# Where the weights of a split-float32 decoder block lie in SBUF: hi 192 bytes further in, everything else on multiples of 512 bytes

## The chip, the cores and the metric

The kernel runs on one core of a Trainium2 chip, with the other cores idle. The metric is the device time of one execution in microseconds (us). Before the change it is 1701.79 us, the median of 3 runs that lay between 1701.62 and 1701.97 us.

## What is computed

One layer of a hybrid decoder block on 256 tokens of width 2048, all in float32. The work is a chain of large products with the stages between them; the weights (about 320 MB) are read from HBM once.

```python
proj = x @ w_in                       # columns: gq gk gv gr glr | fq fk fv ff | ma mb
o  = gla_chunked(q, k, v, log_a)      # branch A: gated linear attention, 4 heads
y_gla = (rmsnorm(o) * silu(gr)) @ w_branch_gla
of = fox_attention(fq, fk, fv, log_f) # branch B: softmax attention with forget bias, 8 heads
y_fox = of @ w_branch_fox
x = layer_norm(ALPHA * x + (sigmoid(ma) * y_gla + sigmoid(mb) * y_fox) @ w_out)
g = causal_dwconv(x @ w_gate, conv_w, conv_b)
x = layer_norm(ALPHA * x + (gelu(g) * (x @ w_up)) @ w_down)
x = x + sigmoid(x @ w_ple_gate) * (p @ w_ple_proj)
```

## The kernel before

**Split numbers.** TensorE multiplies in float32r. So that the result keeps float32's accuracy, each operand is split into a rounded part `hi` and a remainder `lo = raw - hi`, and a product is three: weight-hi by x-hi, weight-hi by x-lo, and weight-lo by x-hi. A tile of activations holds both parts side by side: `a[:, kt%4, 0:256]` is hi of 256 tokens, `256:512` is lo.

**Units of weights.** All weights but the first stage's come in 284 units `u` of 128 x 2048, each as two halves of 128 x 1024. `prep()` makes a half: SyncE's queue (SP) loads it into `raw` (a ring of 4), ScalarE copies it into `hi` (L101), VectorE subtracts to make `lo` (L127). `unit()` hands out the next unit and keeps three prepared ahead. There are 6 places for `hi` and 6 for `lo`. Only SP and a few stretches of TensorE follow an order written out by hand; the other engines' order is the scheduler's.

**Two ways to multiply.** Where *weights are stationary* (176 units: fq, fk, gq, gk, ma, mb, the branch projections, gate and up; tiles `psfq psfk psq psk psm psa psb psg psu`), `w_unit` loads 128 columns of hi into the array, streams 512 columns of activations through them (L190), loads 128 columns of lo and streams 256 (L192): one pair for each 128 rows of the product, 16 pairs a unit. Nearly all of them, 173 units with 2768 pairs, run so; the first three of gate and up go by `w_phase`, 256 columns at a time. Where *activations are stationary* (108 units, `u` in 32-63, 120-135 and 224-283: gv, gr, `wo`, `dn`, `pg`), `x_mm` loads 128 columns of activations for each matmul and streams 512 columns of weights: for each of 128 rows of the product and each half of the tokens x-hi by hi (two matmuls), x-hi by lo (two), x-lo by hi (two), all at L234. That makes 24 matmuls a unit, 2592 in all; the last `pg` bank takes 256 columns at a time in its 96. In both ways every matmul has a weight load of its own, which TensorE takes while the matmul before it runs (PEld in the profile).

**The first stage** makes fv and two small pieces (glr and ff, 24 columns) with activations stationary from 1048 columns of weights, in three chunks `fch` of 352, 352 and 344 columns that lie behind each other in `fvhi` and `fvlo` (`big` places of 8192 bytes). `fv_prep` loads them into the `raw` ring, 8 units of two halves.

**Where tiles lie.** SBUF has a stretch of bytes in each of the 128 partitions; pools are laid out one behind the other in the order of the code. A weight load reads 128 columns of 4 bytes, which is 512 bytes, and a row of an activation tile is 2048 bytes, so a tile's place modulo 512 bytes is that of all its blocks. In the built programs the places modulo 512 are:

| tiles | before | after |
|---|---|---|
| hi, weights stationary | 0 | 192 |
| hi, activations stationary | 0 | 0 |
| lo | 64 | 0 |
| activations, pw, pTs, vs, fvhi, fvlo (`big`) | 0 | 0 |
| hT10, the last of dn's 11 activation tiles (`late`) | 128 | 0 |
| chunks of the first stage's weights | 0, 384, 256 | 0, 0, 0 |
| raw ring, four places | 0, 96, 192, 288 | 0, 0, 0, 0 |
| t1, t2 (small work tiles; ath and atl, the stationary tiles of `go`, among them) | 384 | 0 |
| ones | 64 | 416 |

Of the kernel before, what the change touches and what calls it, by code (L numbers as in the profile page):

```python
# [9 lines left out]
F32 = mybir.dt.float32  # L10
F32R = mybir.dt.float32r
# [8 lines left out]
P = 128  # L20
# [6 lines left out]
FH = 8  # L27
# [5 lines left out]
NS = 1048  # L33
# [4 lines left out]
AFF_DVE = (0, 2)  # L38
LN_ORDER = (1, 0, 3, 2)
GROWS = 96  # L40
PAD = 88
S8W = 2048

OFF = dict(gq=0, gk=1024, gv=2048, gr=4096, glr=6144, fq=6160, fk=7184, fv=8208,
           ff=9232, ma=9240, mb=11288)
# [3 lines left out]
def tile_block(ctx: ExitStack, tc: tile.TileContext, wu, wfv, wpp, xT_in, x_in, pT_in, wlr,  # L49
# [1 line left out]
    nc = tc.nc  # L51

    cst = ctx.enter_context(tc.tile_pool(name="cst", bufs=1))
    wide_hi = ctx.enter_context(tc.tile_pool(name="wide_hi", bufs=6))
    step = ctx.enter_context(tc.tile_pool(name="step", bufs=1))
    gap0 = step.tile([P, 16], F32, name="gap0")
    wide_lo = ctx.enter_context(tc.tile_pool(name="wide_lo", bufs=6))
    step2 = ctx.enter_context(tc.tile_pool(name="step2", bufs=1))
    gap1 = step2.tile([P, 112], F32, name="gap1")
    big = ctx.enter_context(tc.tile_pool(name="big", bufs=15))  # L60
    ring = ctx.enter_context(tc.tile_pool(name="ring", bufs=4))
    sm = ctx.enter_context(tc.tile_pool(name="sm", bufs=2))
# [6 lines left out]
    chn = cst.tile([P, chan.shape[1]], F32, name="chn")  # L69
    ident = cst.tile([P, P], F32, name="ident")  # L70
    mhalf = cst.tile([P, 1], F32, name="mhalf")
    pad = cst.tile([P, PAD], F32, name="pad")

    def s8(shape, dt=F32, name=None):
        t = big.tile([P, S8W], dt, tag="S8", name=name)
        n = int(np.prod(shape[1:]))
        t = t[:shape[0], :n]
        if len(shape) == 3:
            return t.rearrange("p (a b) -> p a b", b=shape[2])
        if len(shape) == 4:  # L80
            return t.rearrange("p (a b c) -> p a b c", b=shape[2], c=shape[3])
        return t

    def w_tile(tag, dt, name):
        pool = wide_hi if tag == "hi" else wide_lo
        return pool.tile([P, 1024], dt, tag=tag, name=name)

    def t1(name):
        return sm.tile([P, 256], F32, tag="t1", bufs=6, name=name)

    def t2(name):
        return sm.tile([P, 512], F32, tag="t2", bufs=6, name=name)

    def mmtile(name):
        return pmm.tile([P, 512], F32, tag="mm", name=name)
# [4 lines left out]
    def copy(o, i, scale=1.0):  # L100
        nc.scalar.activation(o, i, AF.Copy, bias=0.0, scale=scale)  # L101
# [15 lines left out]
    def prep():  # L117
        u = n_prep[0]
        n_prep[0] += 1
        his, los = [], []  # L120
        for h in range(2):
            raw = ring.tile([P, 1024], F32, tag="raw", bufs=4, name=f"raw{u}_{h}")
            nc.sync.dma_start(raw, wu[u, :, h * 1024:(h + 1) * 1024])
            hi = w_tile("hi", F32R, f"hi{u}_{h}")
            copy(hi, raw)
            lo = w_tile("lo", F32R, f"lo{u}_{h}")
            nc.vector.tensor_tensor(lo, raw, hi.bitcast(F32), ALU.subtract)  # L127
            his.append(hi)
            los.append(lo)
        ready[u] = (his, los)  # L130
# [4 lines left out]
    def unit():  # L135
        u = n_used[0]
        n_used[0] += 1
        while n_prep[0] < min(NU, u + 3):
            prep()
        return ready.pop(u)  # L140
# [161 lines left out]


    fv = s8([P, 2, 1024], name="fv")
    fch = ((0, 352), (352, 352), (704, 344))
    fbk = [[mmtile(f"fv_{t}{c}") for c in range(3)] for t in range(2)]

    def fv_prep(u, hs=(0, 1), his=None, los=None):
        his, los = his or [], los or []
        for h in hs:  # L310
            raw = ring.tile([P, NS], F32, tag="raw", bufs=4, name=f"fvraw{u}_{h}")
            hi = s8([P, NS], F32R, name=f"fvhi{u}_{h}")
            lo = s8([P, NS], F32R, name=f"fvlo{u}_{h}")
            for o, n in fch if u == 0 else ((0, NS),):
                e = slice(o, o + n)
                nc.sync.dma_start(raw[:, e], wfv[u, :, h, e])
                copy(hi[:, e], raw[:, e])
                nc.vector.tensor_tensor(lo[:, e], raw[:, e], hi[:, e].bitcast(F32), ALU.subtract)
            his.append(hi)
            los.append(lo)  # L320
        return his, los

    load_x(0, 0, 1, 1)
    f0 = fv_prep(0, (0,))
    load_x(0, 1, 2, 1)
    fvu = [fv_prep(0, (1,), *f0)]
    load_x(0, 2, 4)
    fvu.append(fv_prep(1))
    load_x(1, 0, 4)
    for u in range(8):  # L330
        hi, lo = fvu[u]
        for j in range(2):
            kt = 2 * u + j
            a = xT[kt // 4][:, kt % 4, :]
            for cs in ((0,), (1,), (2,)) if u == 0 else ((0, 1, 2),):
                for t in range(2):
                    ah, al = a[:, t * P:t * P + P], a[:, 256 + t * P:256 + t * P + P]
                    for i, (w, x) in enumerate(((hi[j], ah), (lo[j], ah), (hi[j], al))):
                        for c in cs:
                            o, n = fch[c]  # L340
# [20 lines left out]
    for t in range(2):  # L361
        tk = t1("smtok")
        nc.gpsimd.memset(tk, 0.0)
        for i in range(3):
            copy(tk[:, 32 * i:32 * i + 16], fbk[t][2][:, 320:336])
        copy(tk[:, P:P + FH], fbk[t][2][:, 336:344])
        nc.tensor.transpose(smp[:GROWS, t * P:t * P + P], tk[:, 0:GROWS], ident)
        nc.tensor.transpose(smp[:FH, 256 + t * P:256 + t * P + P], tk[:, P:P + FH], ident)
    for t in range(2):
# [147 lines left out]
    for nm, dst, sc in (("fq", fq, P ** -0.5), ("fk", fk, 1.0)):  # L517
        if nm == "fk":
            mixers.append(fox_gen())
        for n in range(8):  # L520
            hi, lo = unit()
# [8 lines left out]
    for nm, dst, sc in (("q", gq, 1.0 / 16.0), ("k", gk, 1.0)):  # L530
        for n in range(8):
            hi, lo = unit()
            ps = mmtile(f"ps{nm}{n}")
            w_unit(ps, hi, lo, xT, range(16), True, True)
            h, c = n // 2, n % 2
# [163 lines left out]
    for n in range(32):  # L699
        hi, lo = unit()  # L700
# [7 lines left out]
        pull(1)  # L708
    early.close()
    late = ctx.enter_context(tc.tile_pool(name="late", bufs=1))  # L710


    mT = [s8([P, 4, 512], F32R, name=f"mT{i}") for i in range(4)]
    fhl = None
    for n in range(16):
        hi, lo = unit()
# [162 lines left out]
        return banks  # L879

    z1 = [s8([P, 2048], name=f"z1{t}") for t in range(2)]
    st1 = [sm.tile([P, 4, 6], F32, tag=f"st1{t}", bufs=1, name=f"st1{t}") for t in range(2)]
    gain = [None, None]

    def mid1():
# [82 lines left out]
    tc.keep_in_program_order(nc.scalar.preload_act_table_set("gelu_apprx_tanh_and_others"))  # L968


    gp = [late.tile([P, 264], F32, name=f"gp{i}") for i in range(2)]
    for i in range(2):
        nc.gpsimd.memset(gp[i][:, 0:2], 0.0)
    hT = [None] * 11
# [12 lines left out]
    for n in range(NF):  # L987
# [17 lines left out]
        u = t1("up")  # L1005
# [6 lines left out]
            pull(1)  # L1012

    z2 = [s8([P, 2048], name=f"z2{t}") for t in range(2)]
    st2 = [sm.tile([P, 4, 6], F32, tag=f"st2{t}", bufs=1, name=f"st2{t}") for t in range(2)]

    def mid2():
        for t in range(2):
# [127 lines left out]
```

## Time and profile before

| what | value |
|---|---|
| median of 3 runs | 1701.79 us |
| the profiled execution | 1702.23 us, span 1699.5 us from first to last instruction |
| TensorE matmul busy | 1690.2 us, 99% of the span |
| TensorE weight loads busy | 1456.4 us, 86% |
| VectorE / ScalarE / GpSimd busy | 65% / 49% / 2% |
| DMA queues' share of 16 engines | 58.8% for SP's queue, mean 194 GB/s |
| granted TensorE clock | full all through |

How to read it: the duration of a matmul in a row (392 ns for one of 512 columns) is longer than the distance from its start to the next one's, since matmuls overlap in the array; what one costs is the distance between starts. In a timeline, rows of like matmuls that follow each other are merged with their count (x4), and the distance is the start of the next row less the start of this one, by the count. In a table of stretches, the number of matmuls (x433) takes in those that reach over an edge; as a matmul lasts less than twice the distance of two starts, two are taken off before dividing.

### The profile page before, as it was taken

The numbers are of one execution on the slowest core, as the hardware profiler recorded it, in microseconds if no ns is written. First come the engines' busy times: TensorE is split into PE (matmuls) and PEld (weight loads), VectorE is DVE, ScalarE is ACT, GpSimd is POOL, SyncE is SP. The second block draws the span as 40 slices with busy tenths as digits, with TensorE's granted clock in tenths as the row PEclk, the third lists the DMA queues.
The fourth block names the chain that finished last, engine by engine and source line by source line (L and its number), as shares of the span: only waits on it lengthen the run. The fifth ranks groups of instructions, "written<-read, shape, count | busy, mean of one in ns | idle before, by whom it ended". The sixth has DMA issues, their size and how long they took to land.

```text
span 1699.5 us, 23843 instructions
## 1 busy us (share of the span) xinstructions
PE 1690.2 (99%) x9035; PEld 1456.4 (86%) x9035; DVE 1098.0 (65%) x1588; ACT 833.9 (49%) x1200; POOL 36.7 (2%) x123
## 2 busy tenths in 40 slices
PE   9999999999999999999999999999999999999998
PEld 8888888888888888888888888888888888888787
DVE  6666658758756547774687776666666644544774
ACT  5655545445555544443365445445445433334633
POOL 0100000000000000000010000000000000000000
PEclk9999999999999999999999999999999999999999
DMA  7765555555555556557656665555555575566455
GB/s 266 260 198 166 165 185 180 178 175 178 181 174 173 162 187 192 190 189 281 220 165 197 215 215 191 192 190 188 188 195 188 191 287 189 187 194 199 158 175 172
DMA packets 91427, 330.22 MB, mean 194 GB/s; under 512 B 10232, under 2 KB 11904, under 8 KB 89904
## 3 DMA queue, kind: packets, MB, share of 16 engines
q1 hardware_dynamic: 90528, 324.51, 58.8%
q0 software_dynamic: 784, 4.20, 0.7%
q8 instruction: 70, 1.15, 0.3%
q14 instruction: 45, 0.37, 0.1%
HBM read 323.42 MB, written 5.25 MB: 193 GB/s over the span
## 4 chain that ended last, share of the span: by engine, by line
PE 98%; DVE 1%; ACT 0%; DMA 0%; SPq 0%; issue 0%; POOL 0%; ACTq 0%
PE dn L234 14%; PE psu L190 9%; PE psg L190 9%; PE psm L190 7%; PE gv L234 5%; PE gr L234 5%; PE pg L234 5%; PE wo L234 5%; PE psu L192 5%; PE psg L192 5%; PE psm L192 4%; PE psa L190 3%; PE fv L341 2%; PE psa L192 2%; PE psq L190 2%; PE psfk L190 2%
## 5 line engine op out<-in xcount | busy, mean ns | idle before, releaser
L127 DVE TENSOR_TENSOR lo<-raw,hi 128x1024 fp32r<-128x1024 f32 x568 | 694.2, 1224 | 506.9 <-ACT hi L101 505.7
L101 ACT ACTIVATE hi<-raw 128x1024 fp32r<-128x1024 f32 x568 | 601.7, 1060 | 732.6 <-issue 274.7
L190 PE MATMUL psu<-x1T,hi 128*128 128x512 f32 x688 | 240.4, 392 | 0.0
L190 PE MATMUL psg<-x1T,hi 128*128 128x512 f32 x672 | 234.8, 392 | 0.0
L192 PE MATMUL psu<-x1T,lo 128*128 128x256 f32 x688 | 192.3, 280 | 0.0
L234 PE MATMUL dn<-hi,hT 128*128 128x512 f32 x704 | 192.1, 392 | 0.0
L192 PE MATMUL psg<-x1T,lo 128*128 128x256 f32 x672 | 187.8, 280 | 0.0
L190 PE MATMUL psm<-xT,hi 128*128 128x512 f32 x512 | 179.8, 395 | 0.0
L234 PEld LDWEIGHTS dn<-hi,hT 128*128 128x128 f32 x704 | 132.1, 188 | 30.6
L190 PEld LDWEIGHTS psu<-x1T,hi 128*128 128x128 f32 x688 | 129.2, 188 | 27.6
L190 PEld LDWEIGHTS psg<-x1T,hi 128*128 128x128 f32 x672 | 126.2, 188 | 27.0
L192 PE MATMUL psm<-xT,lo 128*128 128x256 f32 x512 | 143.2, 280 | 0.0
L192 PEld LDWEIGHTS psu<-x1T,lo 128*128 128x128 f32 x688 | 130.6, 190 | 0.0
L192 PEld LDWEIGHTS psg<-x1T,lo 128*128 128x128 f32 x672 | 127.6, 190 | 0.0
L190 PEld LDWEIGHTS psm<-xT,hi 128*128 128x128 f32 x512 | 96.2, 188 | 21.2
L234 PE MATMUL dn<-lo,hT 128*128 128x512 f32 x352 | 111.9, 395 | 0.0
L192 PEld LDWEIGHTS psm<-xT,lo 128*128 128x128 f32 x512 | 97.0, 189 | 0.2
L190 PE MATMUL psa<-oT,hi 128*128 128x512 f32 x256 | 89.5, 392 | 0.0
L234 PEld LDWEIGHTS dn<-lo,hT 128*128 128x128 f32 x352 | 66.1, 188 | 14.8
L234 PE MATMUL gv<-hi,xT 128*128 128x512 f32 x256 | 72.6, 395 | 0.0
L234 PE MATMUL gr<-hi,xT 128*128 128x512 f32 x256 | 72.4, 395 | 0.0
L192 PE MATMUL psa<-oT,lo 128*128 128x256 f32 x256 | 71.6, 280 | 0.0
(247 smaller groups left out, 2435.2 us busy)
## 6 DMA issues: line engine op xcount, KB each, us to landing
raw<-in_wu_dram SPq DMA_DIRECT2D x568, 512.0 KB, 4.6
fvraw<-in_wfv_dram SPq DMA_DIRECT2D x14, 524.0 KB, 6.5
lnb<-in_lng_dram SPq DMA_DIRECT2D x4, 1024.0 KB, 13.3
z<-in_x_dram SPq DMA_DIRECT2D x2, 1024.0 KB, 9.5
praw<-in_wpp_dram SPq DMA_DIRECT2D x4, 512.0 KB, 4.5
x1d<-z POOLq DMA_DIRECT2D x2, 1024.0 KB, 7.6
z<-x1d SPq DMA_DIRECT2D x2, 1024.0 KB, 9.6
xraw<-in_xT_dram SPq DMA_DIRECT2D x7, 256.0 KB, 7.1
```

What stands on the lines that cost most here:

```text
L101: nc.scalar.activation(o, i, AF.Copy, bias=0.0, scale=scale)
L127: nc.vector.tensor_tensor(lo, raw, hi.bitcast(F32), ALU.subtract)
L190: nc.tensor.matmul(ps, lhsT=hi[i // 8 if hoff == 0 else 0][:, w0 % 1024:w0 % 1024 + P], rhs=a[:, kt % 4, :], start=first and i == 0, stop= ...
L192: nc.tensor.matmul(ps[:, 256:512], lhsT=lo[i // 8 if hoff == 0 else 0][:, w0 % 1024:w0 % 1024 + P], rhs=a[:, kt % 4, 0:256], start=False, ...
L234: nc.tensor.matmul(bs[j][:, 0:m], lhsT=x, rhs=v[:, o:o + m], start=first and i == 0, stop=last and i == 2)
L341: nc.tensor.matmul(fbk[t][c][:, 0:n], lhsT=x, rhs=w[:, o:o + n], start=kt == 0 and i == 0, stop=kt == 15 and i == 2)
```

## The change

One pool `wide` takes the place of two with gaps between them. A place for hi is now 1152 columns (4608 bytes) instead of 1024, and `w_tile` puts hi's 1024 columns 48 columns (192 bytes) into it unless `u` is in `XSTAT`, the units with activations stationary. lo, `big`, the ring, t1 and t2 come to 0 modulo 512. The first stage's raw rows move from the ring into hi's six places, its chunks become 384, 384 and 280 columns. Small tiles move so that all fits: statistics st1 and one of st2 to the constants, the convolution's rows gp into two of the six t2 places.

```diff
--- before.py
+++ after.py
...
-PAD = 88
+PAD = 16
+LPAD = 24
+XSTAT = (*range(32, 64), *range(120, 136), *range(224, 284))
 S8W = 2048
+WH = 1152
+HSTEP = 48
...
-    wide_hi = ctx.enter_context(tc.tile_pool(name="wide_hi", bufs=6))
-    step = ctx.enter_context(tc.tile_pool(name="step", bufs=1))
-    gap0 = step.tile([P, 16], F32, name="gap0")
-    wide_lo = ctx.enter_context(tc.tile_pool(name="wide_lo", bufs=6))
-    step2 = ctx.enter_context(tc.tile_pool(name="step2", bufs=1))
-    gap1 = step2.tile([P, 112], F32, name="gap1")
+    wide = ctx.enter_context(tc.tile_pool(name="wide", bufs=6))
     big = ctx.enter_context(tc.tile_pool(name="big", bufs=15))
...
+    st1 = [cst.tile([P, 4, 6], F32, name=f"st1{t}") for t in range(2)]
+    st20 = cst.tile([P, 4, 6], F32, name="st20")
     pad = cst.tile([P, PAD], F32, name="pad")
...
-    def w_tile(tag, dt, name):
-        pool = wide_hi if tag == "hi" else wide_lo
-        return pool.tile([P, 1024], dt, tag=tag, name=name)
+    def w_tile(tag, dt, name, u):
+        if tag == "lo":
+            return wide.tile([P, 1024], dt, tag=tag, name=name)
+        o = 0 if u in XSTAT else HSTEP
+        return wide.tile([P, WH], dt, tag=tag, name=name)[:, o:o + 1024]
...
-    fch = ((0, 352), (352, 352), (704, 344))
+    fch = ((0, 384), (384, 384), (768, 280))
...
-            raw = ring.tile([P, NS], F32, tag="raw", bufs=4, name=f"fvraw{u}_{h}")
+            raw = wide.tile([P, WH], F32, tag="hi", name=f"fvraw{u}_{h}")[:, 0:NS]
...
-            copy(tk[:, 32 * i:32 * i + 16], fbk[t][2][:, 320:336])
-        copy(tk[:, P:P + FH], fbk[t][2][:, 336:344])
+            copy(tk[:, 32 * i:32 * i + 16], fbk[t][2][:, 256:272])
+        copy(tk[:, P:P + FH], fbk[t][2][:, 272:280])
...
     late = ctx.enter_context(tc.tile_pool(name="late", bufs=1))
+    late.tile([P, LPAD], F32, name="lpad")
...
-    st1 = [sm.tile([P, 4, 6], F32, tag=f"st1{t}", bufs=1, name=f"st1{t}") for t in range(2)]
...
-    gp = [late.tile([P, 264], F32, name=f"gp{i}") for i in range(2)]
+    gp = [t2(f"gp{i}")[:, 0:264] for i in range(2)]
...
-    st2 = [sm.tile([P, 4, 6], F32, tag=f"st2{t}", bufs=1, name=f"st2{t}") for t in range(2)]
+    st2 = [st20, sm.tile([P, 4, 6], F32, tag="st2", bufs=1, name="st21")]
```

No instruction is added or taken away. In the order of the instructions two things are to be seen. The first is SP's queue in the first stage: `fvraw1_0` is unit 1's first half, and what stands in brackets is what SP waits for before it issues that load. Before:

```order
L316 DMA fvraw1_0_168<-in_wfv_dram 128x1048 [waits DMAHW1_49]
L316 DMA fvraw1_1_174<-in_wfv_dram 128x1048 [waits DMAHW2_49]
L149 DMA xraw_180<-in_xT_dram 128x512 [waits DMAHW3_49]
L149 DMA xraw_184<-in_xT_dram 128x512 [waits DMAHW4_49]
L316 DMA fvraw2_0_224<-in_wfv_dram 128x1048 [waits DMAHW5_49,DVE_49]
L316 DMA fvraw2_1_230<-in_wfv_dram 128x1048 [waits DMAHW7_49,DMAHW6_49,DVE_49]
```

After:

```order
L319 DMA fvraw1_0_160<-in_wfv_dram 128x1048 [waits DMAHW1_49]
L319 DMA fvraw1_1_166<-in_wfv_dram 128x1048 [waits DMAHW2_49]
L152 DMA xraw_172<-in_xT_dram 128x512 [waits DMAHW3_49]
L152 DMA xraw_176<-in_xT_dram 128x512 [waits DMAHW4_49]
L319 DMA fvraw2_0_216<-in_wfv_dram 128x1048 [waits DMAHW5_49]
L319 DMA fvraw2_1_222<-in_wfv_dram 128x1048 [waits DMAHW6_49]
```

The order of the loads is the same; unit 2's two loads no longer wait for VectorE to have let go of unit 0's rows, since there are six places instead of four.

The second is TensorE in the first stage, where one stationary block of xT0 meets the three chunks (banks fv_00, fv_01, fv_02 for the first half of the tokens, fv_10 to fv_12 for the second). Before:

```order
L341 MATMUL fv_00_126<-fvhi1_0_169,xT0_111 128x352
L341 MATMUL fv_01_127<-fvhi1_0_169,xT0_111 128x352
L341 MATMUL fv_02_128<-fvhi1_0_169,xT0_111 128x344
L341 MATMUL fv_10_129<-fvhi1_0_169,xT0_111 128x352
L341 MATMUL fv_11_130<-fvhi1_0_169,xT0_111 128x352
```

After:

```order
L344 MATMUL fv_00_118<-fvhi1_0_161,xT0_103 128x384
L344 MATMUL fv_01_119<-fvhi1_0_161,xT0_103 128x384
L344 MATMUL fv_02_120<-fvhi1_0_161,xT0_103 128x280
L344 MATMUL fv_10_121<-fvhi1_0_161,xT0_103 128x384
L344 MATMUL fv_11_122<-fvhi1_0_161,xT0_103 128x384
```

The sequence stands; the widths of the chunks differ, 1048 columns in both. In the rest of the program the rows of TensorE, VectorE, ScalarE and SP stand as before, and on GpSimd the two short clears of gp come behind the four stores `ppd` instead of ahead of them.

More of the change, by code (lines that the diff above doesn't have):

```diff
@@ L123, in prep @@
             nc.sync.dma_start(raw, wu[u, :, h * 1024:(h + 1) * 1024])
-            hi = w_tile("hi", F32R, f"hi{u}_{h}")
+            hi = w_tile("hi", F32R, f"hi{u}_{h}", u)
             copy(hi, raw)
-            lo = w_tile("lo", F32R, f"lo{u}_{h}")
+            lo = w_tile("lo", F32R, f"lo{u}_{h}", u)
             nc.vector.tensor_tensor(lo, raw, hi.bitcast(F32), ALU.subtract)
```

## The prediction

> **What bounds the kernel now.** The page first: span, busy times, and the chain that ended last.
>
> ```profile
> span 1699.5 us, 23843 instructions
> PE 1690.2 (99%) x9035; PEld 1456.4 (86%) x9035; DVE 1098.0 (65%) x1588; ACT 833.9 (49%) x1200; POOL 36.7 (2%) x123
> PEclk9999999999999999999999999999999999999999
> PE 98%; DVE 1%; ACT 0%; DMA 0%; SPq 0%; issue 0%; POOL 0%; ACTq 0%
> ```
>
> TensorE is busy for all but 9.3 us at a full clock, and the chain is TensorE's own. So nothing another engine does faster is worth anything; the time is 9035 matmuls by the distance between their starts. The change touches no matmul's work but where its operands lie. The next view is therefore the table of stretches, TensorE alone, which gives that distance by stage: gv and gr with the mixers between them, `wo`, gate and up, the first and the second half of `dn`, `pg`.
>
> ```profile
> core 0: us, PE busy (x), PEclk, DMA share, GB/s
> 250.00:424.00 174.00, 173.99 (x812) 1.00 0.56 177
> 765.00:840.00 75.00, 75.00 (x325) 1.00 0.75 263
> 900.00:1300.00 400.00, 400.00 (x2310) 1.00 0.61 196
> 1360.00:1460.00 100.00, 100.00 (x433) 1.00 0.68 231
> 1480.00:1580.00 100.00, 100.00 (x437) 1.00 0.64 205
> 1610.00:1650.00 40.00, 40.00 (x174) 1.00 0.50 174
> ```
>
> Gate and up: 400 us by 2308 is 173.3 ns, so a pair (512 and 256 columns) takes 346.6 ns. With activations stationary, each of 512 columns: `wo` 75/323 = 232.2 ns, `dn` 100/431 = 232.0 in its first half but 100/435 = 229.9 in its second, `pg` 40/172 = 232.6. The two halves of `dn` run the same instructions on the same kinds of tiles, under like DMA load, at two rates. So the distance isn't a constant of the shape; something beside the columns is paid, and it varies. The timeline shows where. First the fast half of `dn`, then the slow half:
>
> ```profile
> 1560.91 1.07 PE L234 MATMUL dn<-hi,hT 128*128 128x512 f32 x4
> 1561.82 0.63 PE L234 MATMUL dn<-lo,hT 128*128 128x512 f32 x2
> 1562.29 0.39 PE L234 MATMUL dn<-hi,hT 128*128 128x512 f32 x1
> ...
> 1400.28 1.09 PE L234 MATMUL dn<-hi,hT 128*128 128x512 f32 x4
> 1401.21 0.62 PE L234 MATMUL dn<-lo,hT 128*128 128x512 f32 x2
> 1401.66 0.62 PE L234 MATMUL dn<-hi,hT 128*128 128x512 f32 x2
> ```
>
> In the fast half four streams of hi (place 0, as the stationary hT) take 0.91 us, 227.5 ns each; two of lo (place 64) take 0.47, 235 ns each. In the slow half hi takes 0.93/4 = 232.5 and lo 0.45/2 = 225. Both halves settle on a rhythm that repeats with the six matmuls of a block; with hi and lo at different places the good one makes lo pay, the bad one makes hi pay.
>
> **The change part by part.**
>
> *Activations stationary: lo from 64 to 0.* All streams then stand as the four hi do. What does a run with both at 0 cost when nothing else comes between? The projection `pp` is one (pw and pTs are both in `big`), and it stands between transposes:
>
> ```profile
> 855.75 2.98 PE L234 MATMUL pp<-pw,pTs 128*128 128x512 f32 x12
> 858.58 0.60 PE L807 MATMUL ptl<-ident,z 128*128 128x128 f32 x4
> 858.93 1.64 PE L234 MATMUL pp<-pw,pTs 128*128 128x512 f32 x6
> 860.41 0.40 PE L203 MATMUL psg<-x1T,hi 128*128 128x256 f32 x2
> ```
>
> Twelve take 2.83 us (235.8 ns each), six take 1.48 (246.7 each). Each run opens with a slow matmul after the transposes; the six that the longer has more cost 1.35 us, 225 ns each. So such a run is dear at its start and 225 to 228 later on. I take 227.5, the row of `dn` itself: `dn` now at 231.0 on the mean of its halves, 1056 x 3.5 ns = 3.7 us less; `wo` 384 x 4.7 = 1.8; `pg` 336 x 5.1 = 1.7. gv and gr (768) have a mixer's small matmuls between every unit or so, and each starts the run anew: I price them like the second half of `dn`, 2.4 ns, and halve it, 768 x 1.2 = 0.9. Together -8.1 us. Bounds: 225 throughout gives 6.0, 7.2, 7.6 and, unhalved, 4.9 ns, so -15.4 us; if a run never settles and costs 235.8, it is +12 us (4.8 ns on 1056, 3.6 on 384, 3.2 on 336, and 5.9 on 768 over 229.9). I stay with the value of `dn`, since its units follow each other for hundreds of matmuls.
>
> *Weights stationary: lo from 64 to 0, hi from 0 to 192.* Now the load of lo's weights (64) runs beside 512 columns, that of hi's (0) beside 256:
>
> ```profile
> 1000.21 0.39 PE L190 MATMUL psg<-x1T,hi 128*128 128x512 f32 x1
> 1000.44 0.28 PE L192 MATMUL psg<-x1T,lo 128*128 128x256 f32 x1
> 1000.56 0.39 PE L190 MATMUL psg<-x1T,hi 128*128 128x512 f32 x1
> ```
>
> That is 230 ns for the long one and 120 here for the short (346.6 less 230 on the mean, 116.6). After the change the load beside 512 columns is at 0 like the stream, the case that `dn` shows at 227.5. The load beside 256 columns is 192 bytes ahead of the stream. One place of before has that distance: the mixer's `pa<-phl,ones`, with the stream at 384 and the load of `ones` at 64, which is 64 - 384 + 512 = 192.
>
> ```profile
> 253.58 0.39 PE L568 MATMUL pa<-phl,ones 128*128 128x256 f32 x2
> 253.81 0.39 PE L234 MATMUL gv<-hi,xT 128*128 128x512 f32 x1
> ```
>
> Two in 0.23 us, 115 ns each; only the first has that distance (the second's neighbour is xT). So 192 is no worse there than 0 is now, and I leave the short one at 116.6. The pair becomes 344.1, 2.5 ns less; times 2768 pairs -6.9 us. Bounds: 225 + 115 = 340, -18.3 us. On the other side stands a rhythm that the kernel already falls into, for two units after each head's product `go`, whose stationary tiles lie at 384:
>
> ```profile
> 495.90 0.63 PE L657 MATMUL go<-vs,ath 128*128 128x512 f32 x2
> 496.37 0.40 PE L657 MATMUL go<-vs,atl 128*128 128x512 f32 x1
> ...
> 498.71 0.40 PE L190 MATMUL psm<-xT,hi 128*128 128x512 f32 x1
> ...
> 500.12 0.40 PE L190 MATMUL psm<-xT,hi 128*128 128x512 f32 x1
> ```
>
> Four pairs in 1.41 us, 352.5 ns each, and that at the same places of hi and lo as elsewhere. If all pairs fell into it: 2768 x 5.9 = +16.3 us. I take the better value, as the row of the same distance is nearer than one of another start; both ends are kept.
>
> *go.* Its stationary tiles come to 0, and with them the start of that slow rhythm: 4 heads x 2 units x 16 pairs x 5.9 ns = 0.8 us; I count -0.6, and between 0 and -0.8.
>
> *First stage.* Three chunks take what three did: the rows below show 0.47 us for three (352, 352, 344 at 0, 384, 256), which is 0.451 ns a column, beside 227.5/512 = 0.444 at 0.
>
> ```profile
> 30.16 0.63 PE L341 MATMUL fv<-fvlo,xT 128*128 128x352 f32 x3
> 30.63 1.11 PE L341 MATMUL fv<-fvhi,xT 128*128 128x352 f32 x6
> 31.58 0.32 PE L341 MATMUL fv<-fvlo,xT 128*128 128x352 f32 x1
> ...
> 7.21 7.86 SPq L316 DMA_DIRECT2D fvraw<-in_wfv_dram  x4
> ```
>
> Over 96 such threes that would be 96 x 7 ns = 0.7 us less; I count 0, and 0.7 to both sides. The last row is SP, which is held for 7.86 us with units 2 and 3 until VectorE lets go of the ring. Six places let unit 2 start sooner, behind unit 1's loads in the same queue; TensorE's wait there is one row, `PE fv L341 <- ACT fvhi`, of 0.3 us. The first chunk is 9% longer, so the first matmul starts later by some 0.1 us. I count +0.1, between -0.5 and +0.5.
>
> ```profile
> PE fv L341 <- ACT fvhi L101: 0.3, 1, 0.3
> ...
> L910 POOL DMA_DIRECT2D ppd<-ppo x4: 539/546/602, 858.9 to 863.1; - x4
> DMA to landing us min/median/max: 2.3/2.9/8.3
> ...
> L217 DVE TENSOR_TENSOR gp<-psg,tmp x3: 417/419/420, 881.1 to 893.4; 128x256 f32<-128x256 f32 x3
> ```
>
> *gp in t2's places.* VectorE's first write of gp0 now waits for a store `ppd` to land, with the splits of lo queued behind it. The last of the four is issued at 863.1 and lands by 872 even at 8.3 us, and VectorE comes to gp at 881.1: nothing, with 9 us to spare. Were that cover gone, TensorE would still have three prepared units of 5.5 us (16 pairs) before it felt the delay. ScalarE's and VectorE's own operands change their places too; both are busy for 49% and 65%, so even 10% more would stay hidden.
>
> *The sum.* -8.1 - 6.9 - 0.6 + 0.1 = -15.5 us, from the profiled execution's 1702.23 us (span 1699.5 and 2.7 around it) to 1686.7; the median of the runs stands 0.4 below that execution, so 1686.3 us.
>
> [...] In the rows above 512 columns take 225 to 235 ns by place and rhythm, with a weight load beside each. [...]
>
> **The rivals.**
>
> 1. *Only lo's move to 0 counts.* The pair's rhythm stays at 346.6 because the 256 columns with hi at 192 lose what the 512 win. For it: short and long trade in the trace as hi and lo do in `dn`. Against it: 115 ns at that distance. -8.1 - 0.6 + 0.1 = -8.6: 1693.2 us.
> 2. *Slower: hi at 192 puts all pairs into the slow rhythm* of 352.5. For it: that rhythm holds for two whole units once entered, and no row shows pairs with hi at 192. Against it: it came after `go` with 384. +16.3 - 8.1 + 0.1 (no gain at `go`) = +8.3: 1710.1 us. It decides from a pair of 346.6 + 8.0/2768 = 349.5 ns on; below that the change is not slower.
> 3. *Places don't matter*, only the start of a run does: the two halves of `dn` differ at the same places, which speaks for it. Against it: inside one rhythm lo and hi differ steadily by 7.5 ns. Then 1701.9 us, the first stage's +0.1 alone.
>
> That the change doesn't do what it says can be excluded: the built program has hi at 192 and 0 and all else as in the table.
>
> **How the numbers follow.** The forecast, 1686.3 us, has a chance of 0.50, better than its sum (both parts near their lower bounds, down to 1702 - 34 = 1668) included; rival 1 has 0.23, rival 2 0.19, rival 3 0.08. The range: up to 1704 it holds forecast, rivals 1 and 3, 0.81; rival 2's milder half reaches to 1706, where I end it, and at the low end 1672 leaves out only both bounds at once. A measurement of this kernel can tell about 0.2% (3.4 us) from no change. Faster by more than that: 0.50 + 0.23 = 0.73, and a little of rival 2 that lies below break-even, 0.74; within: 0.08; slower: 0.18.
>
> **What would show it.** In the profile after: hi and lo alike at 227 to 228 ns in `dn`, `wo` and `pg` timelines (step 1 right), or one of them still at 235 (wrong); x437 or more in 100 us of `dn` in both halves. In gate and up, 400 us with about 2326 matmuls (344.1 a pair) if step 2 holds, 2310 for rival 1, 2272 for rival 2. No slow pairs after `go`. The forecast falls if a pair takes more than 346.6 or if runs with all at 0 settle above 230.

## The result, and the profile after

The changed kernel takes 1676.1 us, the median of 4 runs (1675.62 to 1679.14), beside 1701.88 us for the kernel before in 4 runs on the same chip (1701.62 to 1703.63): a ratio of 0.984 with a 95% interval of 0.983 to 0.9855, or 25.8 us less. The forecast was 1686.3 us. Of the page after, the span and the engines:

```profile
span 1673.6 us, 23839 instructions
PE 1663.7 (99%) x9035; PEld 1442.6 (86%) x9035; DVE 1097.6 (66%) x1588; ACT 833.7 (50%) x1200; POOL 36.0 (2%) x123
```

The same 9035 matmuls fill 26.5 us less, and the idle rest is 9.9 us where it was 9.3. (The page counts four instructions fewer than before, 23839 for 23843; the counts of the engines are the same.) Nothing was won by waiting less: the matmuls follow each other faster. By stretches (us, TensorE busy, matmuls, clock, DMA share, GB/s): gv and gr, gate and up, and the two halves of `dn`:

```profile
250.00:424.00 174.00, 173.95 (x823) 1.00 0.56 179
900.00:1300.00 400.00, 400.00 (x2355) 1.00 0.60 199
1360.00:1460.00 100.00, 100.00 (x443) 1.00 0.61 203
1480.00:1560.00 80.00, 80.00 (x355) 1.00 0.64 209
```

With two taken off for the edges, gate and up make 2353 matmuls in 400 us, 340.0 ns a pair where it was 346.6. `dn` takes 100/441 = 226.8 ns in its first half and 80/353 = 226.6 in its second; it was 232.0 and 229.9. The timeline of the same kernel shows how a pair, a block of `dn`, and the first pairs after `go` look now (start, duration, instruction):

```profile
1000.25 0.39 PE L193 MATMUL psu<-x1T,hi 128*128 128x512 f32 x1
1000.48 0.28 PE L195 MATMUL psu<-x1T,lo 128*128 128x256 f32 x1
1000.59 0.39 PE L193 MATMUL psu<-x1T,hi 128*128 128x512 f32 x1
...
1400.35 1.07 PE L237 MATMUL dn<-hi,hT 128*128 128x512 f32 x4
1401.25 0.62 PE L237 MATMUL dn<-lo,hT 128*128 128x512 f32 x2
1401.70 0.84 PE L237 MATMUL dn<-hi,hT 128*128 128x512 f32 x3
...
493.92 0.40 PE L193 MATMUL psm<-xT,hi 128*128 128x512 f32 x1
...
494.27 0.39 PE L193 MATMUL psm<-xT,hi 128*128 128x512 f32 x1
...
494.61 0.39 PE L193 MATMUL psm<-xT,hi 128*128 128x512 f32 x1
```

A pair is 0.23 and 0.11 us (340 together). Four streams of hi in `dn` take 0.90 us and two of lo 0.45, 225 each, within the rounding of the 226.7 above: hi and lo are alike. After `go` only the first pair is longer (0.35 us), the next is at 0.34; the two slow units of before are gone.

Adding up the distances from each matmul's start to the next one's over the whole trace, by what it writes, gives the sum of the change in us:

| stage | before | after | difference |
|---|---|---|---|
| activations stationary: `dn`, `wo`, gv, gr, `pg` | 602.5 | 593.2 | -9.4 |
| weights stationary: gate and up (`psg`, `psu`) | 492.2 | 483.2 | -9.1 |
| `psm`, with the units after `go` | 179.2 | 175.2 | -4.0 |
| `psa`, `psb` | 133.1 | 130.6 | -2.6 |
| `psfq`, `psfk`, `psq`, `psk` | 180.4 | 179.1 | -1.2 |
| `go` | 8.4 | 8.3 | -0.1 |
| first stage | 47.8 | 48.1 | +0.4 |

With +0.1 us in the small stages that are left, that is -25.9 of the 26.6 us between the two profiled executions; the rest lies outside the span.

### The profile page after: what moved, and what is told of

Read it like the earlier page. It is cut to its first block, busy times and chain, and to the rows that moved or that the text cites. A ratio compares the mean times of both kernels' runs of the same rounds, so it can differ in the third digit from the quotient of the medians.

```text
span 1673.6 us, 23839 instructions
## 1 busy us (share of the span) xinstructions
PE 1663.7 (99%) x9035; PEld 1442.6 (86%) x9035; DVE 1097.6 (66%) x1588; ACT 833.7 (50%) x1200; POOL 36.0 (2%) x123
## 4 chain that ended last, share of the span: by engine, by line
PE 97%; DVE 1%; ACT 0%; DMA 0%; SPq 0%; issue 0%; POOL 0%; ACTq 0%
PE dn L237 14%; PE psu L193 9%; PE psg L193 9%; PE psm L193 7%; PE gr L237 5%; PE gv L237 5%; PE wo L237 5%; PE pg L237 5%; PE psu L195 5%; PE psg L195 5%; PE psm L195 3%; PE psa L193 3%; PE fv L344 2%; PE psfk L193 2%; PE psq L193 2%; PE psfq L193 2%
## 5 line engine op out<-in xcount | busy, mean ns | idle before, releaser
L193 PE MATMUL psu<-x1T,hi 128*128 128x512 f32 x688 | 236.0, 389 | 0.0
L193 PE MATMUL psg<-x1T,hi 128*128 128x512 f32 x672 | 230.5, 389 | 0.0
L193 PE MATMUL psm<-xT,hi 128*128 128x512 f32 x512 | 175.8, 391 | 0.0
```

Source lines behind the costliest of these rows:

```text
L193: nc.tensor.matmul(ps, lhsT=hi[i // 8 if hoff == 0 else 0][:, w0 % 1024:w0 % 1024 + P], rhs=a[:, kt % 4, :], start=first and i == 0, stop= ...
```

## The experiments

What stays open after one number is why. All kernels below are the changed one with the edit shown. All but the last were run once, in three groups: hi0 to shift64, hi64 to hi384, and hi448 to hi160. One execution of the kernel before stood beside each group: 1705.25, 1702.00 and 1704.56 us. Differences of a few us between groups are therefore not read; the distance between starts in gate and up is (900 to 1300 us of each, two matmuls taken off).

### Which part earns it

**hi0**: hi at 0 everywhere, as lo and all else.

```diff
-HSTEP = 48
+HSTEP = 0
```

> The changed kernel with hi at 0 in every unit (step of 0 instead of 192 bytes), all else as changed. Theory A (the distance between the weights that are loaded and the columns that are streamed sets what a matmul pays, for the 256 columns as for the 512): the 512 columns stay at 227 ns, the 256 go from 113 back to 116.6, a pair takes about 344 ns, some 1687 us. Theory B (hi's 192 bytes are worth nothing, the gain came from lo's move from 64 to 0 alone): a pair stays at 340 ns, 1676 us. Theory C (with all at 0 the pairs settle in the slow rhythm of 350 ns or more): 1704 us or more. Units with activations stationary stay at 227 ns by all.

1704.84 us: A (1687) and B (1676) fall, and C's slow rhythm is there. The stretch of gate and up, and the rows of `psa` (duration min/median/max, first and last start), of this kernel; then the `psa` row of the changed kernel:

```profile
900.00:1300.00 400.00, 400.00 (x2267) 1.00 0.59 192
...
L193 PE MATMUL psa<-oT,hi x256: 391/391/391, 630.7 to 760.7; 128*128 128x512 f32 x128
```
```profile
L193 PE MATMUL psa<-oT,hi x256: 389/389/389, 623.5 to 751.0; 128*128 128x512 f32 x128
```

A pair takes 400/2265 x 2 = 353.2 ns in gate and up, but in `psa` and `psb` the same matmuls fill 130.0 us where the changed kernel needs 127.5, which is 340.0 x 130.0/127.5 = 346.7 ns. hi, lo and activations stand at the same places modulo 512 in both stages. So one set of places has more than one steady rhythm, which C didn't have. `psm` shows both with the same kinds of tiles: behind the first head's `go` 16 pairs take 5.65 us, 353 ns each,

```profile
498.43 0.40 PE L193 MATMUL psm<-xT,hi 128*128 128x512 f32 x1
...
504.08 0.40 PE L193 MATMUL psm<-xT,hi 128*128 128x512 f32 x1
```

and the next two units, from 510.6 us on, run at 347. That the way a run begins selects the rhythm fits this, but no run here shows how. The whole gain of the weights-stationary part hangs on hi's 192: with lo at 0 alone, gate and up would have become slower than before.

**hi192all**: hi at 192 for activations stationary too.

```diff
-XSTAT = (*range(32, 64), *range(120, 136), *range(224, 284))
+XSTAT = ()
```

> The changed kernel with hi at 192 in every unit, also where activations are stationary. Theory A: there the stream of hi now stands 192 bytes ahead of the loaded activations and pays as lo at 64 did before, 230 to 235 ns instead of 227 on two of three matmuls: about 1728 x 3 to 8 ns, 1681 to 1690 us, the pairs unchanged at 340 ns. Theory B (only the place of lo matters): 1676 us.

1687.07 us, A's side. `dn` in its first half, by the table of stretches and the timeline:

```profile
1360.00:1460.00 100.00, 100.00 (x434) 1.00 0.64 217
```
```profile
1399.74 1.09 PE L237 MATMUL dn<-hi,hT 128*128 128x512 f32 x4
1400.66 0.62 PE L237 MATMUL dn<-lo,hT 128*128 128x512 f32 x2
1401.12 1.08 PE L237 MATMUL dn<-hi,hT 128*128 128x512 f32 x4
```

100/432 = 231.5 ns against 226.8; hi takes 0.92/4 = 230 and lo, which was not moved, 0.46/2 = 230. Here a stream at 192 costs some 4.7 ns a matmul, and the matmuls between pay with it. Added up over the trace, the stages with activations stationary take 603.4 us, 10.2 more than in the changed kernel. That is most of the 11.6 us by which this run is longer than shift64, below, which has the changed kernel's time, in the same group. With activations stationary, hi at 0 like lo is worth 10.2 us; the forecast had 8.1 for lo's move.

**swap**: with weights stationary, hi at 0 and lo at 192 (the first stage's raw rows then go to lo's places).

```diff
-        if tag == "lo":
+        if tag == "hi":
...
-            raw = wide.tile([P, WH], F32, tag="hi", name=f"fvraw{u}_{h}")[:, 0:NS]
+            raw = wide.tile([P, WH], F32, tag="lo", name=f"fvraw{u}_{h}")[:, 0:NS]
```

> The changed kernel with the parts exchanged where weights are stationary: hi at 0, lo at 192, so that the load 192 bytes ahead runs beside the 512 columns and the load at 0 beside the 256. (The first stage's raw rows lie in lo's places then.) Theory A: the 512 columns pay, 230 to 235 ns, the 256 take 116.6, a pair 347 to 352 ns, 1695 to 1709 us. Theory D (what counts is only that the two loads stand apart by 192): a pair takes 340 ns, 1676 us.

1695.42 us. The stretch, then a pair:

```profile
900.00:1300.00 400.00, 400.00 (x2310) 1.00 0.59 196
```
```profile
1000.48 0.40 PE L193 MATMUL psg<-x1T,hi 128*128 128x512 f32 x1
1000.71 0.28 PE L195 MATMUL psg<-x1T,lo 128*128 128x256 f32 x1
1000.82 0.40 PE L193 MATMUL psg<-x1T,hi 128*128 128x512 f32 x1
```

A pair is 346.6 ns, as before the change, and not 340: it matters which of the two loads stands 192 bytes in. The long matmul takes 346.6 - 113 = 233 ns, the short one 0.11 us. A's direction is right, its split between the two is not: the short one stayed as cheap as in the changed kernel although the load beside it is now at 0. Nor is the distance between hi and lo what counts: modulo 256 bytes, the period found below, the step from lo to hi is 192 in the kernel before (64 and 0) as in the changed one (0 and 192), and a pair takes 346.6 and 340.

**shift64**: everything behind the constants moves by 64 bytes, all distances stay.

```diff
-PAD = 16
+PAD = 32
```

> The changed kernel with everything behind the constants shifted by 64 bytes: hi at 256 or 64, lo, activations and all other tiles at 64 modulo 512; every distance between tiles is kept. Theory A (distances decide): as changed, 340 ns a pair, 227 ns with activations stationary, 1676 us. Theory E (the place itself decides, a multiple of 512 being the good one): 230 ns or more with activations stationary, 346 ns a pair, 1695 to 1705 us.

1675.47 us, the changed kernel's time, with its rhythms in the long stages:

```profile
900.00:1300.00 400.00, 400.00 (x2355) 1.00 0.60 199
1360.00:1460.00 100.00, 100.00 (x443) 1.00 0.63 206
```

So, for this shift of 64 bytes, it is not the place of a tile that counts but its distance to what is read beside it (A): 340.0 ns a pair and 226.8 in `dn`, as in the changed kernel. The distances alone don't fix the rhythm, though: the sixth to eighth unit of `psfq` and the first of `psfk` run at 340 ns here and at 350 in the changed kernel, and three other units (one of `psfk`, two of `psm`) the other way round.

### Which distances are good

The next seven change only `HSTEP`, hi's step in bytes over four: the distance between the weights of hi and the columns streamed while they load.

**hi64** and **hi128** (`HSTEP = 16` and `HSTEP = 32`).

> The changed kernel with hi 64 bytes in (instead of 192) where weights are stationary. Theory F (a pair's rhythm depends on hi's distance itself): 64 is near 0, where pairs took 346.7 to 353.3 ns, so 344 ns or more a pair, 1687 us or more. Theory G (any distance that isn't 0 breaks the bad rhythm): 340 ns, 1676 us.

> As before it, hi 128 bytes in. Theory F: between 0 and 192, 340 to 347 ns a pair, 1676 to 1695 us. Theory G: 340 ns, 1676 us.

**hi256** and **hi384** (`HSTEP = 64` and `HSTEP = 96`), the same at two larger steps.

> hi 256 bytes in. Theory F: at 192 or better if the cost falls on to the middle of the 512 bytes, 333 to 340 ns a pair, 1657 to 1676 us. Theory G: 340 ns, 1676 us.

> hi 384 bytes in, which is 128 behind the stream. [...] Theory G: 340 ns, 1676 us.

(In the kernel before, whose stationary tiles of `go` lie at 384, the matmuls of `go` stand 229 to 239 ns apart.) The four gave 1701.02, 1708.75, 1704.43 and 1709.42 us. Gate and up of hi64, hi128, hi256 and hi384, in this order:

```profile
900.00:1300.00 400.00, 400.00 (x2287) 1.00 0.60 194
```
```profile
900.00:1300.00 400.00, 400.00 (x2275) 1.00 0.59 193
```
```profile
900.00:1300.00 400.00, 400.00 (x2266) 1.00 0.59 192
```
```profile
900.00:1300.00 400.00, 400.00 (x2275) 1.00 0.59 193
```

Pairs of 350.1, 352.0, 353.4 and 352.0 ns. F is borne out by 64, and 128 is worse than it said. G falls at all four. At 256 F is wrong too: that kernel behaves like hi0, 353.4 in gate and up and again 130.0 us for `psa` and `psb`; and 384 behaves like 128. That suggested a theory that had not been stated, H: the distance counts modulo 256 bytes.

**hi448** (`HSTEP = 112`), which is 192 modulo 256, tests it:

> The changed kernel with hi 448 bytes in where weights are stationary. Theory H (what counts is the distance modulo 256 bytes, since 256 gave the rhythms of 0 and 384 those of 128): 448 is 192, so 340 ns a pair and 1676 us. Theory I (192 is good modulo 512 alone): 448 is 64 behind the stream, 344 ns a pair or more, 1687 us or more.

1677.45 us:

```profile
900.00:1300.00 400.00, 400.00 (x2354) 1.00 0.60 199
```

340.1 ns a pair. H holds: the three pairs of distances that differ by 256 (0 and 256, 128 and 384, 192 and 448) agree within 0.2 ns in gate and up.

**hi224** and **hi160** (`HSTEP = 56` and `HSTEP = 40`), the neighbours of 192.

> hi 224 bytes in, half a step of 64 further. Theory J (the places fall into stretches of 64 bytes, and a block may begin anywhere in its stretch): 340 ns, 1676 us. Theory K (192 is a narrow optimum, as its neighbours 128 and 256 are both bad): 346 ns a pair or more, 1692 us or more.

> hi 160 bytes in, half a step of 64 nearer. Theory J: the stretch of 128 to 191, so 352 ns as with 128, about 1708 us. Theory K: 346 ns a pair or more, 1692 us or more.

1692.99 and 1702.12 us; gate and up of hi224, then of hi160:

```profile
900.00:1300.00 400.00, 400.00 (x2324) 1.00 0.59 197
```
```profile
900.00:1300.00 400.00, 400.00 (x2291) 1.00 0.59 194
```

344.5 and 349.5 ns. J falls at both; K is nearer, but the 344.5 lies between what the two gave, and hi224 has `psa` at 629.4 to 759.4 us in its trace, 346.7 ns there. Stretches of 64 bytes are not the rule. Of the distances tried, 192 (and 448) is the only one at which gate and up run at 340 ns, and none of the theories says why; 32 and 96 were not tried.

The 340 ns are not 192's alone. In hi64, which has 350 in gate and up, 12 of the 32 units of `psm` run at 340, among them those behind `go`; here 30 pairs in 10.20 us:

```profile
500.35 0.39 PE L193 MATMUL psm<-xT,hi 128*128 128x512 f32 x1
...
510.55 0.39 PE L193 MATMUL psm<-xT,hi 128*128 128x512 f32 x1
```

So hi 64 and 192 bytes in have the same two rhythms, 340 and 350 ns, and differ in the one that most stages take.

### The units that stayed slow

The changed kernel still has some 200 pairs at 350 ns: six units in a row from the sixth of `psfq` to the third of `psfk`, the first of them behind the small transposes `pct`, and then two of `psfk` and every second one of `psq`, each right behind the logits `pl` of the fox branch, and one of `psk` behind transposes. Not every logit does it: the unit behind the one at 119.6 us runs at 340. The timeline at a slow one:

```profile
144.69 0.82 PE L459 MATMUL pl<-fk,fq 128*128 128x128 f32 x4
145.16 0.58 PE L193 MATMUL psfk<-xT,hi 128*128 128x512 f32 x1
...
145.69 0.40 PE L193 MATMUL psfk<-xT,hi 128*128 128x512 f32 x1
...
147.44 0.40 PE L193 MATMUL psfk<-xT,hi 128*128 128x512 f32 x1
```

**logits_order** exchanges the two products of a logit, so that the narrow one, of 128 columns, comes last instead of the one of 256.

```diff
             pl = mxtile(f"pl{h}")
-            for t, (o, n) in enumerate(halves):
+            for t, (o, n) in reversed(list(enumerate(halves))):
```

> The changed kernel; in the mixer of the forgetting attention the two products of logits change places, so that the one of 128 columns comes last instead of the one of 256. In the changed kernel the units after logits run pairs of 350 ns to their end and those after values, whose last product has 128 columns, run 340. Theory L (what ends just before a run of pairs decides its rhythm): the units after logits go to 340 ns, some 130 pairs by 10 ns, 1.3 us less than the changed kernel, about 1675 us. Theory M (the rhythm there comes from what the other engines do meanwhile): 350 ns stays, 1676 us.

1680.38 us, the median of 4 runs (1677.76 to 1681.77); against the kernel before beside it (1703.26) a ratio of 0.9859, 0.984 to 0.9879. Its timeline behind a logit:

```profile
132.98 0.82 PE L459 MATMUL pl<-fk,fq 128*128 128x256 f32 x4
133.56 0.47 PE L193 MATMUL psfk<-xT,hi 128*128 128x512 f32 x1
...
133.99 0.40 PE L193 MATMUL psfk<-xT,hi 128*128 128x512 f32 x1
...
134.34 0.40 PE L193 MATMUL psfk<-xT,hi 128*128 128x512 f32 x1
```

Behind the first pair the changed kernel makes five in 1.75 us (145.69 to 147.44), 350 ns each. With the order exchanged the first pair takes 0.43 instead of 0.53 us, the next still 0.35, and so to the end of the unit: L falls. M, that the other engines set the rhythm, isn't shown by that. What the pairs win, the logits lose (0.8 us each over the trace). The kernel isn't faster either, and the reason is elsewhere, in `wo` (rows of TensorE's timeline, with the wait in brackets):

```profile
802.09 1.10 PE L237 MATMUL wo<-hi,mT 128*128 128x512 f32 x2 [1.98 <-DVE z L838]
...
803.49 1.57 PE L237 MATMUL wo<-hi,mT 128*128 128x512 f32 x4
804.85 1.06 PE L237 MATMUL wo<-lo,mT 128*128 128x512 f32 x2
805.70 1.82 PE L237 MATMUL wo<-hi,mT 128*128 128x512 f32 x4
807.37 0.63 PE L237 MATMUL wo<-lo,mT 128*128 128x512 f32 x2
```

TensorE waits 2 us for VectorE's residual `z`, and behind the wait ten matmuls take 3.88 us (803.49 to 807.37), 388 ns each: together some 3.6 us. All in all `wo` takes 91.7 us instead of 87.4, and `psfq` 46.0 instead of 44.4, by a second stretch at half clock (told at the end); these two make up what the span is longer than the changed kernel's (5.7 us). VectorE is late since ScalarE is (it waits 9.84 us for ScalarE's `hi`, 7.15 in the changed kernel), and ScalarE since a load of weights is. ScalarE's timeline of this kernel, then of the changed one, with its wait for that load in brackets:

```profile
788.09 1.06 ACT L104 ACTIVATE hi<-raw 128x1024 fp32r<-128x1024 f32 x1 [10.00 <-DMA raw<-in_wu_dram]
```
```profile
784.40 1.06 ACT L104 ACTIVATE hi<-raw 128x1024 fp32r<-128x1024 f32 x1 [7.32 <-DMA raw<-in_wu_dram]
```

Four loads of 1 MB, two of the residual's rows `z` and two of the layer norm's constants, stand in SP's queue ahead of that point (767.9 to 772.6 us in the two traces). The changed kernel has no wait in `wo`; hi0, swap, hi128, hi160, hi224 and hi384 have one of 0.2 to 1.2 us at this place, which their times contain. So the stage has little room left. Why the load came later here than in the changed kernel, the runs don't show.

## Why the prediction was right, and where not

**What bounds the kernel.** Right. The busy share of TensorE is still 99%, idle time didn't fall, and the whole difference is in the distance between starts.

**Activations stationary.** Forecast -8.1, measured -9.4 us: `dn` -4.4 (3.7 forecast), `wo` -1.8 (1.8), gv and gr -2.3 (0.9), `pg` -0.9 (1.7; its matmuls stand 229.3 ns apart on the mean). The run does settle where hi already was, at 226.7 rather than 227.5 ns, for hi and lo alike. Halving the gain for gv and gr was too careful. hi192all, with hi moved away again and lo left at 0, loses all of it: what counts is the common place.

**Weights stationary.** This is the term that was mis-sized: -6.9 forecast, -16.1 us measured (the table's -16.9 without the 0.8 of the units after `go`). A pair fell to 340.0 ns, the lower bound that the working had named (225 + 115), not to 344.1. The failing step was to price each matmul by the one load beside it: the short one was left at 116.6 because 192 was thought no worse there than 0. It took 113, and the long one 227, as forecast. (6.6 ns on 2768 pairs would be 18.3 us; some 200 pairs at 350 keep 2 of them.) And the prices don't add: with the load beside the long matmul at 0 in both kernels, the changed one takes 340 and hi0 353, while swap has the short one at 113 beside a load at 0. What has a price, as far as these runs go, is the pattern of the pair. The row of `pa` at the same distance was the right one to look at, and its 115 ns should have entered the sum instead of standing beside it.

**go, first stage, gp.** `go` and what follows it: forecast -0.6, measured about -0.9 (4 x 2 units x 16 pairs by 5.9 ns, and 0.1 of its own). The size was right by luck, for the mechanism wasn't: hi0 and swap have the stationary tiles of `go` at 0 too, and the two units behind it run at 353 and 350 ns there. So moving `go`'s tiles doesn't end the slow start; in the changed kernel it went with hi's 192. First stage: +0.1 forecast, +0.4 measured, inside its bounds; the wait for `fvhi`, 0.3 us before, is 0.7. No wait for gp shows in the trace.

**The rivals.** The first, that hi at 192 earns nothing for the pair, fell: 340 against 353 or 347 in hi0. The second, the slow rhythm for all pairs, is real, but at other distances: 64, 128 and 160 give 349.5 to 352 ns. With a step of 128 or 384 bytes the single runs are 6.8 and 7.4 us above the kernel before beside them, the rival's 8.3 nearly. The third fell most clearly: with the same instructions in the same order, `HSTEP` alone moves the time from 1677 to 1709 us, and a pair in gate and up from 340 to 353 ns. But its case for the start of a run has something to it: hi0 and hi64 each hold two rhythms at one set of places.

**What stays open.** Why 192 modulo 256 is good and 224, 32 bytes on, is not; and what chooses between 353 and 347 (hi0) or 350 and 340 (hi64, and behind the logits); that it is the start of a run is argued. Only one start was changed, the logits' order, and the rhythm stayed. Each kernel has one trace, so whether a rhythm comes back in every execution isn't shown. No kernel tried beats the change: shift64 and hi448 are level with it in single runs.

## What to carry to other kernels

When TensorE is busy all the time, its time is the distance between starts: divide a stretch by its matmuls, stage by stage, and where like shapes differ, look at where the operands lie. With a weight load beside every matmul, try the distance between the loaded weights and the streamed columns as a number to be measured, through all steps of 32 or 64 bytes within 256, and price whole patterns (a pair, a block of six), not single matmuls. The same distance can run in a good and in a bad rhythm (340 and 350 ns at 64 and at 192 bytes here), so look at every stage, and at its first units, before a distance is called good.

## What the runs showed of the hardware

In gate and up, steps of hi that differ by 256 bytes gave the same pair, though a weight load reads 512 bytes of a partition (128 columns of 4 bytes): 353.2 and 353.4 ns at 0 and 256, 352.0 and 352.0 at 128 and 384, 340.0 and 340.1 at 192 and 448. The same places held two rhythms for hundreds of matmuls (353 and 347 ns in hi0, 350 and 340 in hi64).

Behind the wait of 1.98 us in logits_order the matmuls lost almost as much again. The stretches around it:

```profile
803.00:804.00 1.00, 1.00 (x6) 0.94 0.88 254
804.00:805.00 1.00, 1.00 (x4) 0.50 0.41 164
...
806.00:807.00 1.00, 1.00 (x4) 0.50 0.00 0
807.00:808.00 1.00, 1.00 (x5) 0.85 0.00 0
```

From 804 to 807 us the granted clock is 0.50 with TensorE busy, so ten matmuls lost another 1.6 us (388 against 227 ns each). The half clock came about 1.8 us after they had begun again (802.09 us; the mean clock is 0.98 from 803.5 to 803.9 and 0.50 from 803.9 to 807.0). That the wait brought it on was not shown.

Earlier in this run the clock is halved without a long wait; before it lie three pauses of 0.38, 0.94 and 0.43 us, within 3.5 us:

```profile
56.40:59.80 3.40, 3.40 (x12) 0.50 0.66 205
```

The changed kernel has the same pauses (0.38, 0.94 and 0.43 us, between 53.2 and 56.7 us) at full clock. So what brings the half clock on stays open. The mean granted clock is 0.999 in hi64, hi128, hi160, hi192all, hi224 and hi448 too, and 0.998 in hi384; as an estimate, a thousandth is 1.7 us of a run of 1700 us.
